# Fourteen instead of twelve chunk pairs in a seven-product down projection, with the rooms, the issue order and the final-norm products rearranged around it

## The chip, the cores and the metric

The kernel runs on one core of one Trainium2 chip. The metric is the device time in microseconds (us) of one execution; the figure given for a kernel is the median of its runs. The engines are TensorE (PE, matrix products; PEld is its weight load), VectorE (DVE, elementwise), ScalarE (ACT, elementwise with functions), GpSimd (POOL) and SyncE (SP); here SP issues most of the loads from memory and POOL issues a few.

## The reference

The reference is one decoder layer over 272 tokens (16 learned ones and 256 of input) of 2048 features. Cut to what matters here:

```python
h = h + y @ w_out                          # after attention and retention
u = rmsnorm(h, ffn_norm)
g = causal_conv3(u @ w_gate)               # 2048 -> 5632
a = silu(g) * (u @ w_up)                   # 5632 features
h = h + a @ w_down                         # 5632 -> 2048, "down"
out = rmsnorm(h, final_norm)[last 256 tokens]
```

All of it is float32. The kernel gets that accuracy from a reduced-precision matrix type by splitting each operand into a high and a low half and adding three products: high by high, high by low, low by high.

## The kernel before, in words

The work runs in stages: 48 input projections with attention and retention beside them, 16 output projections, then "gate and up" (for each of the NF = 44 chunks of 128 features one gate product and one up product, with convolution, silu and the product of the two), and last "down". Every weight chunk is loaded by SP into a `raw` tile (five places, used in turn, L166 to L172). `prep` (L191) then makes its two halves: ACT copies the weight to the high half (L206, tiles `whi`), DVE subtracts that from the weight to give the low half (L207, tiles `wlo`). There are four places for such a pair of halves: three of `whi`/`wlo` and one called `wx`. So part n of the weights can be split only when PE is done with part n-4. PE uses the halves in L872, L873 and L874.

Down multiplies 2 halves of the tokens (m = 0, 1; 128 tokens each) by 44 feature chunks by 4 column blocks of 512. It does the column blocks two at a time, in two groups g = 0, 1; a group holds its partial sums in the eight banks of PSUM. There are two ways to do the feature chunks of a group:

* A plain part `W` is two feature chunks for one column block: 1024 weight columns to split, and 4 products of 512 columns (2 token halves by 2 chunks).
* A pair of feature chunks is done with seven products of 128x128x512 instead of eight, as in Strassen's method for two-by-two blocks. The weights of a pair come as four parts: `d` (two blocks as loaded, two products), `u` (two sums of blocks, two products), `t` (the two blocks of `d`, each less one of the sums, two products) and `c` (one block, called B11, one product). So a pair splits 3584 weight columns, and DVE also does the subtraction of 1024 columns that makes `t` (L218).

NS = 12 pairs cover feature chunks 0 to 23; the other 20 are plain. `down_order` (L96) writes the order of a group out by hand: some plain parts first (4 in group 0, 2 in group 1), then the 48 parts of the pairs with plain parts spread evenly between them, then the rest of the plain parts (3 in group 0, 8 in group 1). The last HOLD = 6 plain parts of group 1 are held: they are multiplied for the first token half, then for the second, so that the first half's result can be finished meanwhile.

What a pair needs beside the weights is made in the gate and up stage. `stage` (L777) loads three weight blocks of a pair on POOL's queue into a tile `ts`, `sums` (L786) makes the two sums `td` of them with two DVE instructions and stores them to memory. For each pair of chunks, L831 to L843 make sums of activations, split them and store them to memory (`sd`). In down, the load of a pair (L174 to L184) issues four transfers on SP, in this order: the two blocks of `d`, the activation sums `sf`, the sums `td`, and B11 (`sw`). `sf` and `sw` each have two rooms, used in turn by even and odd pairs; a room is part of the memory that held the activations of the earlier stage (`act2a` to `act3b`).

At each part, `ahead` (L229) issues the loads of chunks that open up to 6 parts later and the splits of parts up to 3 later, then the products follow, and then `pump` takes one task from the list `side` (three at a time behind the last pair). Those tasks are the additions of the PSUM banks into the result `htok` (L925), the squares for the final norm (`square`, L893, on ACT), the products with the final norm's weights (`weigh`, L899, on DVE), and the load (`norm`, L853, on POOL's queue, a transfer of 512 KB) and scaling (`norm_scale`, L859) of these weights for one group's columns. Before the change, the tasks that finish group 0 run among the first parts of group 1: four squares, four `weigh`, then `norm(1)` and, 12 parts later, `norm_scale(1)`.

The order in which each engine gets its instructions is settled when the kernel is built: the compiler's scheduler takes the instructions by their place in the program, but lets one go ahead when it expects an earlier one to wait. Instructions inside `keep(...)` stay in the order of the program among themselves. On the chip, each engine then takes its instructions strictly in that order.

Of the kernel before, what the change touches and what calls it, by code (L numbers as in the profile page):

```python
# [44 lines left out]
LAM_INIT = 0.8 - 0.6 * math.exp(-0.3 * 0)  # L45
HK = KT // 2
HOLD = 6
NS = 12
KP = 2 * NS
NPL = (NF - KP) // 2  # L50
LEAD = [(4, 3), (2, HOLD + 2)]
PARTS = ("d", "u", "t", "c")
ROOMS = (0, 1, "2a", "2b", "3a", "3b")
RSEQ = [("y", 0), ("g", 0), ("y", 1), ("g", 1), ("y", 2), ("y", 3), ("g", 2), ("g", 3)]


# [60 lines left out]
def trunk_kernel(ctx, tc, a, out):  # L117
# [48 lines left out]
    def load(c):  # L166
        turn = (c - nw) % 5 if c >= nw else 0
        if turn == 3:
            t = pools["dn"].tile([P, D], F32, tag="sraw", name=f"raw{c}")
        elif turn == 4:  # L170
            t = big.tile([P, D], F32, tag="act1", name=f"raw{c}")
        else:  # L172
            t = wp.tile([P, D], F32, tag="raw", bufs=3, name=f"raw{c}")
        if c in mixed:  # L174
            g, p = divmod(mixed[c], NS)
            sf = big.tile([P, 6 * P], F32R, tag=f"act{2 + p % 2}a", name=f"sf{g}_{p}")
            sw = big.tile([P, NW], F32, tag=f"act{2 + p % 2}b", name=f"sw{g}_{p}")
            w = a["w_mix"][g, p]
            keep(nc.sync.dma_start(out=t[:, :2 * NW], in_=w[:, :2 * NW]))
            keep(nc.sync.dma_start(out=sf.bitcast(F32), in_=pools["sd"][p]))  # L180
            keep(nc.sync.dma_start(out=t[:, 2 * NW:], in_=pools["td"][g, p]))
            keep(nc.sync.dma_start(out=sw, in_=w[:, 2 * NW:3 * NW]))
            pools["sf"][g, p] = sf
            pools["sw"][g, p] = sw  # L184
        else:
            ins = nc.sync.dma_start(out=t, in_=chunks[c])
            if c >= nw:
                keep(ins)
        raw[c] = t

    def prep(hf):  # L191
        c, s = entries[hf]
        held = len(entries) - 1 - hf
        if held < 2:
            hi, lo = [big.tile([P, 1024], F32R, tag=f"act{2 + held}{i}", name=f"end{held}{i}")
                      for i in "ab"]
        elif c >= nw and (hf - 2 * nw) % 4 == 3:
            wx = big.tile([P, 2 * 1024], F32R, tag="act0", name=f"wx{hf}")
            hi, lo = wx[:, :1024], wx[:, 1024:]
        else:  # L200
            hi = wp.tile([P, 1024], F32R, tag="whi", bufs=3, name=f"whi{hf}")
            lo = wp.tile([P, 1024], F32R, tag="wlo", bufs=3, name=f"wlo{hf}")

        def halves(src, b, e):
            with tc.high_priority() if 8 < hf < 16 else nullcontext():
                S.copy(out=hi[:, b:e], in_=src)  # L206
                V.tensor_tensor(out=lo[:, b:e], in0=src, in1=hi[:, b:e].bitcast(F32),  # L207
                                op=ALU.subtract)

        if c in mixed:  # L210
            g, p = divmod(mixed[c], NS)
            if s == "d":
                halves(raw[c][:, :2 * NW], 0, 2 * NW)
            elif s == "u":
                halves(raw[c][:, 2 * NW:], 0, 2 * NW)
                two = raw[c][:, :2 * NW].rearrange("p (a c) -> p a c", a=2)
                t2 = raw[c][:, 2 * NW:3 * NW].unsqueeze(1).to_broadcast([P, 2, NW])
                V.tensor_tensor(out=two, in0=two, in1=t2, op=ALU.subtract)  # L218
            elif s == "t":
                halves(raw[c][:, :2 * NW], 0, 2 * NW)  # L220
            else:
                halves(pools["sw"][g, p], 0, NW)
        else:
            halves(raw[c][:, s * 1024:(s + 1) * 1024], 0, 1024)
        pairs[hf] = (hi, lo)
        if s in (1, PARTS[-1]):
            raw.pop(c)
# [536 lines left out]
    with ExitStack() as p2:  # L764
# [27 lines left out]
            stage()  # L792

        for f in range(NF):
            if f in (1, 2):
                stage()
            if staged and (f >= KP or f >= 4 and f % 2 == 0):
                sums()
            if f in (39, 41):
                m = (f - 39) // 2  # L800
                halfs.append(big.tile([P, D], F32, tag=f"htok{m}", name=f"htok{m}"))
                keep(nc.sync.dma_start(out=halfs[m], in_=hd[m * P:(m + 1) * P]))
            ps = gemm_q(idx, gs, 0)
# [56 lines left out]
            keep(V.tensor_scalar(out=fns[g], in0=fns[g], scalar1=-0.5, scalar2=None,  # L860
                                 op0=ALU.mult))

        norm(0)
        side.extend([nop] * 12 + [lambda: norm_scale(0)])
        so = sp.tile([P, 2, NB + 1], F32, name="so", bufs=1)
        pre = sp.tile([P, 2], F32, name="pre", bufs=1)
        root = sp.tile([P, 1], F32, name="root", bufs=1)
# [60 lines left out]
        for g in range(2):  # L928
# [42 lines left out]

                return [f1, f2, f3, f4, f5]

            def finish(m, j):
                n = 2 * g + j

                def f():
                    square(m, n * NW, (n + 1) * NW, n)
                    weigh(m, n * NW, (n + 1) * NW)
                return f  # L980

            def take(m, j):
                def f():
# [6 lines left out]
            for i, (kind, x, y) in enumerate(seq):  # L990
                ahead(e)
                if g and i >= len(seq) - HOLD:
                    held.append((y, e))
                    e += 1
                    continue
                wt = pairs[e]
                if kind == "w":
                    for m in range(2):
                        for kk in range(2):
                            product((m, x % 2), acts(m, KP + 2 * y + kk), wt, kk * NW)  # L1000
                elif y == "d":
                    product((0, 0), acts(0, 2 * x + 1), wt, 0)
                    product((0, 1), forms(x, 2), wt, NW)
                elif y == "u":
                    product(6, forms(x, 0), wt, 0)
                    product(7, forms(x, 1), wt, NW)
                elif y == "t":
                    product((1, 0), acts(1, 2 * x + 1), wt, 0)
                    product(5, acts(1, 2 * x), wt, NW)
                else:  # L1010
                    product(1, acts(0, 2 * x), wt, 0)
                pairs.pop(e)
                e += 1
                if i == last_s:
                    side.extend(joined())
                    side.extend([take(0, 0), take(1, 0)])
                    if g:
                        side.extend([finish(0, 0), finish(1, 0)])
                        side.append(lambda: S.activation(out=root, in_=so[:, 1, 2:3],
                                                         func=AF.Sqrt))  # L1020
                pump(3 if i > last_s else 1)
            pump(len(side))
            if not g:
                take(0, 1)()
                take(1, 1)()
                side.extend([nop] * 6)
                for m, j in ((0, 0), (1, 0), (0, 1), (1, 1)):
                    side.extend([finish(m, j), nop, nop])
                side.append(lambda: norm(1))
                side.extend([nop] * 12 + [lambda: norm_scale(1)])  # L1030
                continue
            po = [bank[0, 1], bank[1, 1]]
            nb = NPL
# [121 lines left out]
```

## Time and profile before

| | |
|---|---|
| median of 3 runs | 1151.01 us (1151.01 to 1151.01) |
| profiled execution | 1151.3 us, its span 1149.5 us |
| PE busy | 1138.5 us, 99% of the span |
| DVE busy | 931.0 us, 81% |
| ACT busy | 605.6 us, 53% |
| POOL busy | 36.2 us, 3% |
| moved by DMA | 276.76 MB, mean 241 GB/s |

The span runs from the first to the last instruction that the profile shows; 1.8 us of the execution's own time lie outside it. "Busy" is the time in which an engine has an instruction in work; instructions of one engine can overlap a little at their ends, so the distance from one start to the next is shorter than an instruction's duration. In a list of waits, each row tells which engine and line waited, for whom, how long in total, how many times, and the longest. In a list by stretches, each engine's busy time stands with the number of its instructions in brackets.

### The profile page before, as it was taken

Reading aid. Unit: us, or ns where it says so; the run is one execution under the profiler, and the core shown is the slowest. Engines: PE = TensorE matmul, PEld = TensorE weight load, DVE = VectorE, ACT = ScalarE, POOL = GpSimd, SP = SyncE. Lnnn points to the kernel's source line nnn. Section 1 sums busy time; section 2 is a strip of 40 time slices with the busy share of each in tenths; the row PEclk is TensorE's granted clock in tenths of the full one; section 3 lists DMA queues with packets and bytes.
Section 4 is the critical chain, followed back from the end, with each engine's and each line's share of the span. In section 5 each row is a group of like instructions: output and inputs, shape, how many; then the busy total and the mean of one; then the engine's idle time right before and its main releaser. Section 6 shows DMA issues by size and latency. Waiting matters only on the chain.

```text
span 1149.5 us, 20662 instructions
## 1 busy us (share of the span) xinstructions
PE 1138.5 (99%) x7967; PEld 1065.6 (93%) x7967; DVE 931.0 (81%) x1738; ACT 605.6 (53%) x997; POOL 36.2 (3%) x84
## 2 busy tenths in 40 slices
PE   8999999999999999999999999999999999999997
PEld 7999999999999999999999999999999988888886
DVE  7898787667677769888888888888877778889996
ACT  7676665443345545444544444444444456656663
POOL 0000000000000000000000000100000000000000
PEclk9999999999999999999999999999999999999999
DMA  9644546565648875767867777888876588877981
GB/s 317 211 155 161 180 144 199 167 223 166 203 159 253 238 228 187 284 243 256 288 249 251 273 286 266 289 313 304 310 271 226 193 302 300 287 287 259 315 314 74
DMA packets 96018, 276.76 MB, mean 241 GB/s; under 512 B 43856, under 2 KB 52176, under 8 KB 74160
## 3 DMA queue, kind: packets, MB, share of 16 engines
q1 hardware_dynamic: 87616, 238.08, 59.9%
q0 software_dynamic: 8160, 37.23, 8.9%
q8 instruction: 62, 1.02, 0.3%
q14 instruction: 36, 0.29, 0.1%
q10 hardware_dynamic: 144, 0.14, 0.1%
HBM read 251.56 MB, written 23.86 MB: 240 GB/s over the span
## 4 chain that ended last, share of the span: by engine, by line
PE 98%; DMA 1%; ACT 0%; DVE 0%; issue 0%; SPq 0%; DVEq 0%; ACTq 0%
PE mm L459 14%; PE mm L448 10%; PE mm L446 10%; PE mm L447 10%; PE mm L438 7%; PE mm L439 7%; PE mm L440 7%; PE mm L461 7%; PE o L873 4%; PE o L874 4%; PE o L872 4%; PE x L872 2%; PE x L874 2%; PE x L873 2%; PE po L583 1%; DMA xr<-in_x_dram 1%
## 5 line engine op out<-in xcount | busy, mean ns | idle before, releaser
L206 ACT CAST whi<-raw 128x1024 fp32r<-128x1024 f32 x379 | 397.9, 1051 | 376.3 <-issue 90.7
L207 DVE TENSOR_TENSOR wlo<-raw,whi 128x1024 fp32r<-128x1024 f32 x379 | 462.0, 1222 | 131.6 <-ACT whi L206 124.7
L459 PE MATMUL mm<-g,whi 128*128 128x512 f32 x352 | 124.4, 392 | 0.0
L448 PE MATMUL mm<-g,wlo 128*128 128x258 f32 x352 | 99.4, 282 | 0.0
L438 PE MATMUL mm<-x,whi 128*128 128x272 f32 (+1 forms) x344 | 99.3, 289 | 0.0
L446 PE MATMUL mm<-g,whi 128*128 128x260 f32 x352 | 99.2, 282 | 0.0
L440 PE MATMUL mm<-x,wlo 128*128 128x272 f32 (+1 forms) x344 | 99.0, 288 | 0.0
L439 PE MATMUL mm<-x,whi 128*128 128x272 f32 (+1 forms) x344 | 98.9, 288 | 0.0
L461 PE MATMUL mm<-g,wlo 128*128 128x256 f32 x352 | 98.6, 280 | 0.0
L447 PE MATMUL mm<-g,whi 128*128 128x256 f32 x352 | 97.8, 278 | 0.0
L459 PEld LDWEIGHTS mm<-g,whi 128*128 128x128 f32 x352 | 66.1, 188 | 13.1
L446 PE MATMUL mm<-ys,whi 128*128 128x260 f32 x256 | 71.9, 282 | 0.0
L448 PE MATMUL mm<-ys,wlo 128*128 128x258 f32 x256 | 71.8, 281 | 0.0
L447 PE MATMUL mm<-ys,whi 128*128 128x256 f32 x256 | 70.7, 276 | 0.0
L447 PEld LDWEIGHTS mm<-g,whi 128*128 128x128 f32 x352 | 66.7, 189 | 1.9
L461 PEld LDWEIGHTS mm<-g,wlo 128*128 128x128 f32 x352 | 66.2, 188 | 0.0
L446 PEld LDWEIGHTS mm<-g,whi 128*128 128x128 f32 x352 | 66.1, 188 | 0.0
L448 PEld LDWEIGHTS mm<-g,wlo 128*128 128x128 f32 x352 | 66.0, 188 | 0.0
L439 PEld LDWEIGHTS mm<-x,whi 128*128 128x128 f32 x344 | 64.9, 189 | 0.0
L440 PEld LDWEIGHTS mm<-x,wlo 128*128 128x128 f32 x344 | 64.8, 189 | 0.0
L438 PEld LDWEIGHTS mm<-x,whi 128*128 128x128 f32 x344 | 64.8, 188 | 0.0
L873 PE MATMUL o<-wlo,fhi 128*128 128x512 f32 x149 | 58.0, 389 | 0.0
(404 smaller groups left out, 3060.6 us busy)
## 6 DMA issues: line engine op xcount, KB each, us to landing
raw<-in_w_in_dram SPq DMA_DIRECT2D x44, 1024.0 KB, 5.0
raw<-in_w_gate_dram SPq DMA_DIRECT2D x44, 1024.0 KB, 5.7
raw<-in_w_up_dram SPq DMA_DIRECT2D x44, 1024.0 KB, 5.4
raw<-in_w_down_dram SPq DMA_DIRECT2D x20, 1024.0 KB, 8.4
ts<-in_w_mix_dram POOLq DMA_DIRECT2D x24, 768.0 KB, 5.9
raw<-in_w_out_dram SPq DMA_DIRECT2D x16, 1024.0 KB, 5.3
td<-ts POOLq DMA_DIRECT2D x24, 512.0 KB, 6.6
raw<-in_w_mix_dram SPq DMA_DIRECT2D x24, 512.0 KB, 8.3
```

The costliest lines, as they stand in the source:

```text
L206: S.copy(out=hi[:, b:e], in_=src)
L207: V.tensor_tensor(out=lo[:, b:e], in0=src, in1=hi[:, b:e].bitcast(F32), op=ALU.subtract)
L438: PE.matmul(ps[:, :n], wh, xh, start=(k == 0), stop=False)
L439: PE.matmul(ps[:, :n], wh, xl, start=False, stop=False)
L440: PE.matmul(ps[:, :n], wl, xh, start=False, stop=(k == KT - 1))
L446: PE.matmul(ps[:, :NQ + 2], wh, src.cols(k, GO - 2, GL), start=(k == 0), stop=False)
L447: PE.matmul(ps[:, 4:NQ + 2], wh, src.cols(k, GL, GW), start=False, stop=False)
L448: PE.matmul(ps[:, 2:NQ + 2], wl, src.hi(k), start=False, stop=(k == KT - 1))
L459: PE.matmul(ps, wh, src.cols(k, GO + 2, GW), start=(k == 0), stop=(k == KT - 1))
L461: PE.matmul(ps[:, :SEQ], wl, src.cols(k, GO + 2, GL), start=False, stop=False)
L872: PE.matmul(o, ah, wh, start=start, stop=False)
L873: PE.matmul(o, ah, wl, start=False, stop=False)
```

## The change

`NS` goes from 12 to 14: fourteen pairs, so 28 chunks are paired and 16 are plain. A group then has 56 parts of pairs and 16 plain parts; in group 0 these are 4 in front, 9 between and 3 behind, in group 1 they are 2, 6 and 8.

Around that, four things are rearranged. The activation sums `sf` take three rooms in turn (`act2a`, `act2b`, `act3a`), and the two places of B11 are the halves of one tile in the fourth (`act3b`). The subtraction that makes part `t` moves in the program from behind the split of `u` to behind the split of `d`. In gate and up, the weight sums start at f = 2 and are made at three of every four chunks, and the two loads of the token rows (`htok`) are issued at f = 41 and 42 instead of 39 and 41. And the products with the final norm move: `norm(0)` is issued 24 parts into group 0 instead of before it, the squares of group 0 still run early in group 1, but its four `weigh`, `norm(1)` and `norm_scale(1)` come behind the last pair of group 1.

```diff
-NS = 12
+NS = 14
+FORMS = ("2a", "2b", "3a")
...
             g, p = divmod(mixed[c], NS)
-            sf = big.tile([P, 6 * P], F32R, tag=f"act{2 + p % 2}a", name=f"sf{g}_{p}")
-            sw = big.tile([P, NW], F32, tag=f"act{2 + p % 2}b", name=f"sw{g}_{p}")
+            n = mixed[c]
+            sf = big.tile([P, 6 * P], F32R, tag="act" + FORMS[n % 3], name=f"sf{g}_{p}")
+            if "b11" not in pools:
+                pools["b11"] = big.tile([P, 2, NW], F32, tag="act3b", name="b11")
+            sw = pools["b11"][:, n % 2]
...
             if s == "d":
                 halves(raw[c][:, :2 * NW], 0, 2 * NW)
-            elif s == "u":
-                halves(raw[c][:, 2 * NW:], 0, 2 * NW)
                 two = raw[c][:, :2 * NW].rearrange("p (a c) -> p a c", a=2)
                 t2 = raw[c][:, 2 * NW:3 * NW].unsqueeze(1).to_broadcast([P, 2, NW])
                 V.tensor_tensor(out=two, in0=two, in1=t2, op=ALU.subtract)
+            elif s == "u":
+                halves(raw[c][:, 2 * NW:], 0, 2 * NW)
...
         for f in range(NF):
-            if f in (1, 2):
+            if f < 2:
                 stage()
-            if staged and (f >= KP or f >= 4 and f % 2 == 0):
+            elif staged and f % 4 != 3:
                 sums()
-            if f in (39, 41):
-                m = (f - 39) // 2
+            if f in (41, 42):
+                m = f - 41
...
-        norm(0)
-        side.extend([nop] * 12 + [lambda: norm_scale(0)])
+        side.extend([nop] * 24 + [lambda: norm(0)] + [nop] * 12 + [lambda: norm_scale(0)])
...
-            def finish(m, j):
-                n = 2 * g + j
-
-                def f():
-                    square(m, n * NW, (n + 1) * NW, n)
-                    weigh(m, n * NW, (n + 1) * NW)
-                return f
+            def squared(m, n):
+                return lambda: square(m, n * NW, (n + 1) * NW, n)
+
+            def weighed(m, n):
+                return lambda: weigh(m, n * NW, (n + 1) * NW)
...
                 if i == last_s:
+                    if g:
+                        side.extend([weighed(m, n) for n in range(2) for m in range(2)])
+                        side.append(lambda: norm(1))
                     side.extend(joined())
                     side.extend([take(0, 0), take(1, 0)])
                     if g:
-                        side.extend([finish(0, 0), finish(1, 0)])
+                        side.append(lambda: norm_scale(1))
+                        for m in range(2):
+                            side.extend([squared(m, 2), weighed(m, 2)])
                         side.append(lambda: S.activation(out=root, in_=so[:, 1, 2:3],
                                                          func=AF.Sqrt))
...
                 side.extend([nop] * 6)
-                for m, j in ((0, 0), (1, 0), (0, 1), (1, 1)):
-                    side.extend([finish(m, j), nop, nop])
-                side.append(lambda: norm(1))
-                side.extend([nop] * 12 + [lambda: norm_scale(1)])
+                for m, n in ((0, 0), (1, 0), (0, 1), (1, 1)):
+                    side.extend([squared(m, n), nop, nop])
                 continue
```

## The prediction, made before the changed kernel was built

> **What bounds the kernel now.** I read the page first: the span, the busy lines and the chain of work that ended last.
>
> ```profile
> span 1149.5 us, 20662 instructions
> PE 1138.5 (99%) x7967; PEld 1065.6 (93%) x7967; DVE 931.0 (81%) x1738; ACT 605.6 (53%) x997; POOL 36.2 (3%) x84
> PE 98%; DMA 1%; ACT 0%; DVE 0%; issue 0%; SPq 0%; DVEq 0%; ACTq 0%
> ```
>
> PE carries 98% of the chain, so what counts is how many matrix products PE has and where it waits. The change touches two stages, so the second view is busy time by stretches: gate and up with activation sums (420 to 689) and without (689 to 880), then down: the pairs of group 0 (919 to 1010), the pairs of group 1 (1033 to 1115.25), and from the last pair to the end of the first token half (1115.25 to 1135.40). The two rows of 20 us are parts of group 1.
>
> ```profile
> core 0: us, PE busy (x) PEld busy (x) DVE busy (x) ACT busy (x) POOL busy (x), PEclk, DMA share, GB/s
> 420.00:689.00 269.00, 269.00 (x1922) 252.99 (x1921) 222.37 (x413) 129.83 (x216) 17.17 (x32) 1.00 0.71 256
> 689.00:880.00 191.00, 191.00 (x1361) 179.52 (x1360) 156.68 (x255) 88.33 (x138) 14.39 (x27) 1.00 0.80 289
> 919.00:1010.00 91.00, 91.00 (x403) 75.37 (x402) 75.90 (x73) 54.01 (x59) 0.53 (x1) 1.00 0.85 301
> 1000.00:1020.00 20.00, 20.00 (x90) 16.57 (x89) 17.12 (x17) 13.59 (x15) 0.00 (x0) 1.00 0.92 352
> 1033.00:1115.25 82.25, 82.07 (x359) 66.76 (x358) 74.19 (x73) 52.78 (x59) 0.53 (x1) 1.00 0.84 297
> 1040.00:1060.00 20.00, 19.92 (x87) 15.96 (x86) 19.42 (x22) 12.09 (x14) 0.53 (x1) 1.00 0.82 299
> 1080.00:1100.00 20.00, 19.91 (x87) 15.82 (x86) 19.14 (x19) 12.51 (x15) 0.00 (x0) 1.00 0.94 324
> 1115.25:1135.40 20.15, 20.15 (x100) 17.04 (x99) 18.16 (x25) 11.05 (x15) 0.00 (x0) 1.00 0.16 53
> ```
>
> PE never pauses in gate and up or in group 0. In group 1 it does: two stretches of 20 us hold 87 matrix products where full ones hold 90, and there DVE is busy for over 19 of 20 us. The third view, the waits in down, names them; the three PEld rows (1.7 us in all) are the same in the answer for group 1's pairs alone, so all of them lie there.
>
> ```profile
> ACT whi L206 <- PE o L874: 25.6, 20, 2.5
> ACT whi L206 <- PE x L874: 16.1, 23, 2.2
> ACT whi L206 <- DVE raw L218: 10.7, 7, 2.5
> PEld x L872 <- ACT whi L206: 0.9, 2, 0.5
> ACT end1a L206 <- DMA raw<-in_w_down_dram: 0.8, 1, 0.8
> PEld x L872 <- ACT wx L206: 0.5, 1, 0.5
> ACT wx L206 <- DMA raw<-in_w_down_dram: 0.4, 1, 0.4
> PEld o L872 <- ACT whi L206: 0.3, 1, 0.3
> SPq L180 <- PE x L874: 112.5, 21, 14.0
> ```
>
> ACT mostly waits for PE to free one of the four places (harmless: that is the lead), seven times for the subtraction L218, and hardly for a load. So down is a race: PE first, DVE close behind, with a lead of at most four parts.
>
> **The unit prices.** PE and DVE rows from the timeline; the first two rows are the first product of a plain part and that of the part behind it.
>
> ```profile
> 924.85 0.39 PE L872 MATMUL o<-wx,fhi 128*128 128x512 f32 x1
> 927.57 0.39 PE L872 MATMUL o<-whi,fhi 128*128 128x512 f32 x1
> ...
> 1042.40 0.68 DVE L899 TENSOR_TENSOR htok<-htok,fn 128x512 f32<-128x512 f32 x1
> ...
> 1048.24 1.22 DVE L207 TENSOR_TENSOR wlo<-raw,whi 128x1024 fp32r<-128x1024 f32 x1
> 1049.38 0.68 DVE L207 TENSOR_TENSOR wx<-sw,wx 128x512 fp32r<-128x512 f32 x1
> 1049.98 0.68 DVE L899 TENSOR_TENSOR htok<-htok,fn 128x512 f32<-128x512 f32 x1
> 1050.58 2.35 DVE L207 TENSOR_TENSOR wlo<-raw,whi 128x1024 fp32r<-128x1024 f32 x2
> ...
> 1057.52 0.68 DVE L899 TENSOR_TENSOR htok<-htok,fn 128x512 f32<-128x512 f32 x1
> ...
> 1079.80 0.69 DVE L860 TENSOR_SCALAR fn<-fn 128x1024 f32<-128x1024 f32 x1
> ```
>
> From start to start: a plain part of 12 matrix products takes 2.72 us, so one takes 0.2267. A split of 1024 columns takes DVE 1.14 (1048.24 to 1049.38), one of 512 columns, or a product with the norm, 0.60. I price the subtraction of 1024 columns and the scaling like the rows of their length, 1.14 and 0.60. A pair is then 21 x 0.2267 = 4.76 us of PE and 4 x 1.14 + 0.60 = 5.16 us of DVE; a plain part is 2.72 of PE and 1.14 of DVE. Pairs run DVE behind, plain parts let it catch up.
>
> **The products saved.** Two more pairs in two groups save one product of three matrix instructions each: 12 x 0.2267 = **2.72 us** off PE. The Trainium skill's page "TensorE: Matmul & The Clock Gate", section "Back-to-back issue gap", gives a sustained spacing of 131 ns at 512 columns. By that the saving would be an estimated 1.57 us and the sum 1.1 us worse; these rows are 227 ns apart in a stretch without a wait, and the row decides.
>
> **What pays for it.** DVE work against PE time, over the pairs and the plain parts between them ("room" is what PE's time leaves DVE):
>
> * group 0 before: 12 pairs, 13 plain: PE 92.5, DVE 76.7 + 0.6 (scaling) = 77.3; DVE's room 15.2
> * group 0 after: 14 pairs, 9 plain: PE 91.1, DVE 82.5 + 0.6 = 83.1; room 8.0
> * group 1 before: 12 pairs, 10 plain: PE 84.3, DVE 73.3 + 3.0 (four `weigh`, one scaling) = 76.3; room 8.0
> * group 1 after: 14 pairs, 6 plain: PE 83.0, DVE 79.1; room 3.9
>
> The idle time of DVE measured in group 1 is 82.25 - 74.19 = 8.06, close to the 8.0. A room of 15.2 cost PE nothing, a room of 8.0 cost it 1.7.
>
> Group 1 after: at least 0 new wait, since the work fits. At most: if DVE again loses the same share to waiting (8.06 of 82.25, 9.8%), it needs 79.1 / 0.902 = 87.7, which is 4.7 more than PE has. Seven microseconds of room less brought 1.7 of waiting; 4.1 less again should bring at least as much for each, so 1.7 + 1.0 = 2.7, and more as the room runs out. I take **3.2**. Group 0 after: its room is that of group 1 before, so between 0 and 1.7. Both slow stretches of 20 us have the norm's work in or just in front of them (L899 four times, the first at 1042.40 and the last at 1057.52; L860 at 1079.80), and group 0 has one scaling, so I take **0.6**. The existing waits of **1.7** are counted off, since both groups are priced anew.
>
> The subtraction moved ahead of `u` is part of these figures, not a term beside them. It removes seven waits of ACT (10.7 us) behind which DVE had nothing to split; but no PE wait names L218, so alone it is worth 0 to 1.7. It also puts 1.14 us in front of `u`'s split; queued behind it on DVE are `u`, `t` and `c`, and PE waits for `u` where the lead is already spent. That is a cost of 0 to 1.14 in each pair without lead, and one reason for taking 3.2 and not 2.7.
>
> **The end.** Four `weigh` and one scaling, 5 x 0.60 = 3.0 us, move behind the last pair. Rows of the end before, and the landing of the final-norm transfer:
>
> ```profile
> 1135.38 0.69 DVE L1041 TENSOR_TENSOR htok<-o,htok 128x512 f32<-128x512 f32 x1 [1.99 <-PE o L874]
> ...
> 1141.72 0.42 DVE L1060 TENSOR_TENSOR htok<-oe,htok 128x256 f32<-128x256 f32 x1 [1.47 <-PE oe L874]
> ...
> DMA to landing us min/median/max: 8.2/8.4/8.6
> ```
>
> DVE has 1.99 us free before the first token half's sum, so 1.0 of the 3.0 is over, and all 3.0 if DVE arrives late; behind it 1.47 us are free again before the second half's last sum, which starts the chain to the end. Bounds 0 and 3.0 - 1.47 = 1.5; I take **0.6**. `norm(1)` now waits on POOL for the fourth `weigh` (nothing is queued behind it there) and lands 8.6 us later; DVE has ten additions (6.0) and about six splits (6.8) to do before the scaling that needs it, so it waits for nothing. Of the last loads, the second-last chunk now waits for the place of the last plain chunk among the pairs and the last one is queued behind it on SP, where before only the last one waited so (and ACT 0.8 for it); PE comes to them more than three plain parts later (10.9 us), and the loads in this stage's rows, here and below, land in 4.8 to 8.6: 0, at worst 1.
>
> **What is hidden.** Costs in gate and up and of the transfers:
>
> ```profile
> L789 DVE TENSOR_TENSOR ts<-ts 128x512 f32<-128x512 f32 x24 | 16.5, 687 | 0.5
> L841 DVE TENSOR_TENSOR sh<-sm,sh 128x384 fp32r<-128x384 f32 x12 | 6.6, 548 | 0.0
> L834 DVE TENSOR_TENSOR sm<-ful,sm 128x128 f32<-128x128 f32 x12 | 3.4, 284 | 0.0
> raw<-in_w_mix_dram SPq DMA_DIRECT2D x24, 512.0 KB, 8.3
> raw<-td SPq DMA_DIRECT2D x24, 512.0 KB, 5.8
> sf<-sd SPq DMA_DIRECT2D x24, 384.0 KB, 4.8
> sw<-in_w_mix_dram SPq DMA_DIRECT2D x24, 256.0 KB, 6.5
> ```
>
> Four more weight sums (each this row and its sister L788, alike: 1.37) and two more pairs' activation sums (each about 0.55 + 6 x 0.28) are 10 us of DVE in stretches where it idles 46.6 and 34.3 us and PE never waits; sums at three chunks of four instead of two raise DVE there from 83% to 86%. POOL's transfers, 4 loads and 6 stores more, and the `htok` loads two chunks apart become one apart, on queues that PE does not wait for: 0, and the 10 us in full only if DVE's lead were gone. In down a pair loads 1664 KB and a plain part 512 KB, so group 1 goes from 25.1 to 26.4 MB and 297 to 317 GB/s; the trace has a stretch at 352. Three rooms take away most of the 112.5 us that SP waits for a place of `sf`; as ACT waited 1.2 us for loads and PE never, that is worth 0. `norm(0)` behind 24 parts lands in 8.6 us, and 12 parts last longer: 0.
>
> **The sum**: -2.72 - 1.7 + 3.2 + 0.6 + 0.6 = 0.0. The profiled execution takes 1151.3 (1149.5 of span), 0.3 above the median of 1151.01; at the median I predict **1151.0 us**.
>
> **The rivals.** *The lead holds*: with the subtraction early, the norm's work away and the loads further ahead, DVE loses little, 1.0 in group 1, 0 in group 0 and 0.3 at the end: with -2.72 - 1.7 = -4.42 it is -4.42 + 1.3 = -3.1, **1147.9**. For it: the work fits with 3.9 us to spare, and 1.7 us of present waiting can go. Against: DVE idled 8.06 us in group 1 though it was needed.
>
> *DVE becomes the bound of group 1*, slower: it keeps losing 9.8% to the chain of place, high half, low half, so 4.7 there, 1.7 in group 0, and it comes late to the end, 1.5: -4.42 + 7.9 = +3.5, **1154.5**. It decides from 4.42 + 2.3 = 6.7 us of new waits on. For it: the stretches with over 19 of 20 us busy are just those where PE waits, and the engines' order is fixed in advance, so a misjudged instruction holds up all behind it. Against: part of that idle time is DVE being ahead.
>
> *DVE is the bound already*: then each of the four pairs costs 5.16 - 2 x 1.14 = 2.88 us, 11.5 in all, **1162.5**. The Trainium skill, "Perfetto Trace Analysis", section "Identifying the Most-Contended Engine", would have it so: judge TensorE by its weight loads, here 66.76 of 82.25 (81%), and VectorE by occupancy, here 90%. The trace disagrees: PE's products follow each other without a gap but for 1.7 us.
>
> **How the numbers follow.** Chances: forecast 0.57, lead holds 0.18, DVE the bound 0.23, bound already 0.02. A measurement of this kernel can tell 0.2%, 2.3 us, from no change; the forecast's own range is 1148.7 to 1153.3, that is "same". Faster is the second case, 0.18; slower the last two, 0.25. The range to hold 8 in 10 reaches from the second case's time to the third's: 1148.0 to 1154.6.
>
> **What would show it.** Right: 12 products fewer at 0.227 us; waits of PE for ACT's halves in group 1 of 2 to 4.5 us and under 1.7 in group 0; DVE busy above 93% between group 1's first and last pair; DVE's free time before the first half's sum gone. The waits of ACT for L218 should fall well below 10.7 and SP's for `sf` below 112.5 without moving the time by themselves. Wrong: PE waiting for DVE in gate and up, ACT waiting for loads by more than a few us, or group 1 of pairs with PE waits under 1 us (then faster) or over 5 (then slower).

## The result, and the profile after

The changed kernel takes 1160.92 us (median of 6 runs, 1160.72 to 1161.05), the kernel before in the same series 1151.01 us (6 runs). The ratio is 1.0084, with a 95% interval from 1.0073 to 1.0094: slower by 9.9 us where no change was predicted, and outside the range. The profiled execution of after takes 1161.0 us, its span 1159.2. Two executions at a low granted clock are left out of the ratios below: one of e6 (1879.4 us at 0.557) and one of the kernel before, in the series of e5 to e8 (2215.5 us at 0.935).

The page of after, its span, its busy lines and its chain:

```profile
span 1159.2 us, 20731 instructions
...
PE 1141.7 (98%) x7955; PEld 1062.3 (92%) x7955; DVE 948.0 (82%) x1770; ACT 611.0 (53%) x1009; POOL 41.7 (4%) x94
...
PE 92%; DVE 4%; ACT 2%; issue 1%; DMA 1%; SPq 0%; DVEq 0%; ACTq 0%
```

The twelve matrix products are gone (7967 to 7955), but DVE and ACT now hold 6% of the chain that PE held nearly alone. The first and the last product of down, before and then after:

```profile
916.66 0.39 PE L872 MATMUL o<-whi,fhi 128*128 128x512 f32 x1
...
1141.41 0.28 PE L874 MATMUL oe<-end0a,flo 128*128 128x256 f32 x1
```

```profile
916.52 0.39 PE L875 MATMUL o<-whi,fhi 128*128 128x512 f32 x1
...
1150.92 0.28 PE L877 MATMUL oe<-end0a,flo 128*128 128x256 f32 x1
```

Down went from 224.75 us to 234.40, so the whole loss lies there; what comes ahead of it is no later (916.52 against 916.66) and what comes behind its last product is 0.25 longer. With twelve products fewer it should have been 2.72 shorter: some 12.4 us of new waiting. Below, "PE's waits" are this kind of sum: how much further apart than 0.227 us (0.119 for products half as wide) the starts of consecutive products of down lie, in the profiled execution (differences under 0.03 us are left out). It is 1.1 us before and 13.1 after: 2.6 in group 0, 10.5 from group 1 on.

The stretches of after that answer to those of the prediction (the columns are the same), and one more, 1025 to 1120, which holds nearly the whole of group 1's pairs; then that stretch in the kernel before:

```profile
919.00:1010.00 91.00, 89.97 (x390) 72.42 (x390) 78.82 (x77) 55.64 (x62) 0.54 (x1) 1.00 0.85 306
1033.00:1115.25 82.25, 78.16 (x329) 60.31 (x328) 70.64 (x67) 48.66 (x56) 0.00 (x0) 1.00 0.81 277
1025.00:1120.00 95.00, 90.91 (x384) 70.73 (x383) 82.79 (x83) 56.28 (x68) 0.00 (x0) 1.00 0.77 268
```

```profile
1025.00:1120.00 95.00, 94.82 (x415) 77.29 (x414) 86.94 (x88) 60.68 (x71) 0.53 (x1) 1.00 0.76 269
```

This is not the picture of a DVE that became the bound. In group 1, PE does 31 products fewer in the same 95 us, and DVE is busy for less of it than before, 82.8 us against 86.9, though it has more to do. That is 87% of the stretch, where the prediction expected above 93%. PE and DVE both wait. The waits of after in down, from 905 us to the end, name the place (the last two rows are SP's own queue):

```profile
ACT whi L210 <- DVE raw L220: 28.7, 15, 3.0
...
PEld o L875 <- ACT whi L210: 8.4, 14, 1.3
...
PE o L875 <- ACT whi L210: 3.2, 7, 0.8
PEld o L876 <- DVE wx L211: 1.7, 1, 1.7
...
PEld oe L875 <- DVE htok L928: 1.6, 1, 1.6
...
SPq L186 <- DVE wlo L211: 85.0, 18, 15.0
...
SPq L184 <- PE x L877: 7.9, 7, 3.0
```

The lines have moved by two to four: L210 and L211 are the high and the low half, L220 the subtraction, L875 to L877 the products, L928 the additions, L184 and L186 the loads of the activation sums and of B11. SP no longer waits for a room of the sums (7.9 us, before 112.5), as predicted, though it now stands 85.0 for a place of B11. But ACT's waits for the subtraction, which should have fallen well below 10.7 us, rose to 28.7. The timeline of after shows one of them:

```profile
1069.42 2.36 DVE L211 TENSOR_TENSOR wlo<-raw,whi 128x1024 fp32r<-128x1024 f32 x2 [1.19 <-ACT whi L210]
...
1070.76 1.05 ACT L210 CAST whi<-raw 128x1024 fp32r<-128x1024 f32 x1
...
1071.70 0.69 DVE L211 TENSOR_TENSOR wx<-b,wx 128x512 fp32r<-128x512 f32 x1
...
1072.30 1.22 DVE L211 TENSOR_TENSOR wlo<-raw,whi 128x1024 fp32r<-128x1024 f32 x1
...
1073.44 1.22 DVE L220 TENSOR_TENSOR raw<-raw 128x1024 f32<-128x1024 f32 x1
...
1074.77 2.94 ACT L210 CAST whi<-raw 128x1024 fp32r<-128x1024 f32 x3 [2.96 <-DVE raw L220]
...
1075.84 2.36 DVE L211 TENSOR_TENSOR wlo<-raw,whi 128x1024 fp32r<-128x1024 f32 x2 [1.19 <-ACT whi L210]
1075.86 0.19 PEld L875 LDWEIGHTS o<-whi,fhi 128*128 128x128 f32 x1 [1.26 <-ACT whi L210]
1075.86 0.50 PE L875 MATMUL o<-whi,fhi 128*128 128x512 f32 x1 [0.84 <-ACT whi L210]
```

The second half of the first row is this pair's `d`, split by 1071.78. The subtraction could start then. DVE splits a `c` (1071.70) and the pair's `u` (1072.30) first, and only at 1073.44 subtracts. So `t` is ready for ACT at 1074.66. ACT has stood for 2.96 us by then, with the casts of the next two parts queued behind `t` (the three follow each other without a wait). While ACT casts `t`, DVE has nothing to split and stands 1.19 us; PE runs dry and stands about 1.

In the trace of after the subtraction stands behind `u`'s split in 16 of the 28 pairs (5 in group 0, 11 in group 1; "late" below), in the trace of before in 8 of 24. In the program of after it stands ahead of `u` in all 28. The move in the program did not reach the engine (e8 shows this by undoing it).

### The profile page after: what moved, and what is told of

Read it like the earlier page. It is cut to its first block, busy times and chain, and to the rows that moved or that the text cites. A ratio compares the mean times of both kernels' runs of the same rounds, so it can differ in the third digit from the quotient of the medians.

```text
span 1159.2 us, 20731 instructions
## 1 busy us (share of the span) xinstructions
PE 1141.7 (98%) x7955; PEld 1062.3 (92%) x7955; DVE 948.0 (82%) x1770; ACT 611.0 (53%) x1009; POOL 41.7 (4%) x94
## 4 chain that ended last, share of the span: by engine, by line
PE 92%; DVE 4%; ACT 2%; issue 1%; DMA 1%; SPq 0%; DVEq 0%; ACTq 0%
PE mm L463 14%; PE mm L452 10%; PE mm L450 10%; PE mm L451 10%; PE mm L442 7%; PE mm L443 7%; PE mm L444 7%; PE mm L465 7%; PE o L875 3%; PE o L876 3%; PE o L877 3%; PE x L875 2%; PE x L876 1%; PE x L877 1%; DVE wlo L211 1%
## 5 line engine op out<-in xcount | busy, mean ns | idle before, releaser
L210 ACT CAST whi<-raw 128x1024 fp32r<-128x1024 f32 x383 | 401.2, 1051 | 377.1 <-issue 90.2
L211 DVE TENSOR_TENSOR wlo<-raw,whi 128x1024 fp32r<-128x1024 f32 x383 | 467.2, 1223 | 130.3 <-ACT whi L210 124.6
L463 PEld LDWEIGHTS mm<-g,whi 128*128 128x128 f32 x352 | 66.1, 188 | 13.1
L821 ACT COPY ful<-mm 128x256 f32<-128x256 f32 x44 | 16.4, 373 | 78.2 <-PE mm L463 75.7
```

What stands on the lines that cost most here:

```text
L463: PE.matmul(ps, wh, src.cols(k, GO + 2, GW), start=(k == 0), stop=(k == KT - 1))
```

## The experiments

Two theories went into them. **Order**: the time is lost behind late subtractions. **Room**, the prediction's own: DVE's work comes so near to PE's time that any order would lose. Where "held" is said, the instructions are wrapped in `keep`, so that the scheduler leaves them in the order of the program.

| kernel | late subtractions | PE's waits, us | median, us | ratio to before (95%) |
|---|---|---|---|---|
| before | 8 of 24 | 1.1 | 1151.0 to 1151.5 | 1 |
| after | 16 of 28 | 13.1 | 1160.92 | 1.0084 (1.0073 to 1.0094) |
| e1, held ahead | 0 of 28 | 1.9 | 1149.72 | 0.9986 (0.9977 to 0.9995) |
| e2, 12 pairs | 6 of 24 | 0.2 | 1150.27 | 0.9990 (0.9981 to 0.9999) |
| e3, norm products later | 16 of 28 | 14.1 | 1162.87 | 1.0098 (1.0085 to 1.0112) |
| e4, `t` set free | 28 of 28 | 0.7 | 1147.81 | 0.9972 (0.9961 to 0.9984) |
| e5, held behind | 28 of 28 | 23.5 | 1171.42 | 1.0174 (1.0160 to 1.0188) |
| e6, e1 and more work for DVE | 0 of 28 | 11.4 | 1159.61 | 1.0070 (1.0054 to 1.0086) |
| e7, before, held ahead | 0 of 24 | 1.3 | 1150.29 | 0.9992 (0.9983 to 1.0001) |
| e8, move undone in the program | 16 of 28 | 13.2 | 1161.22 | 1.0085 (1.0066 to 1.0104) |
| e9, e1 with the old norm places | 0 of 28 | 3.8 | 1151.46 | 1.0000 (0.9991 to 1.0009) |
| e10, e1 with two rooms | 0 of 28 | 5.1 | 1153.63 | 1.0018 (1.0009 to 1.0027) |
| e11, e1 with e3's edit | 0 of 28 | 3.4 | 1151.17 | 0.9998 (0.9989 to 1.0007) |
| e12, before, held behind | 24 of 24 | 16.2 | 1169.78 | 1.0159 (1.0142 to 1.0176) |

### e1: the subtraction held ahead of `u`

```diff
-        def halves(src, b, e):
+        def halves(src, b, e, pin=lambda ins: ins):
...
-                V.tensor_tensor(out=lo[:, b:e], in0=src, in1=hi[:, b:e].bitcast(F32),
-                                op=ALU.subtract)
+                pin(V.tensor_tensor(out=lo[:, b:e], in0=src, in1=hi[:, b:e].bitcast(F32),
+                                    op=ALU.subtract))
...
-                V.tensor_tensor(out=two, in0=two, in1=t2, op=ALU.subtract)
+                keep(V.tensor_tensor(out=two, in0=two, in1=t2, op=ALU.subtract))
...
-                halves(raw[c][:, 2 * NW:], 0, 2 * NW)
+                halves(raw[c][:, 2 * NW:], 0, 2 * NW, keep)
```

> The changed kernel with one thing added: the subtraction and u's low split are held in the order in which the program writes them, so that in all 28 pairs the subtraction runs on DVE ahead of u's split (in the changed kernel it ran behind it in 16 of 28). Theory 'order': the new waits are those behind a late subtraction, where ACT cannot cast t; with the subtraction always early PE's waits in down fall from 13 us to 4 or less, ACT's waits for L220 fall from 28.7 us to under 6, and the time is 1150 to 1153.5. Theory 'room': DVE is too full with 28 pairs, whatever the order; the waits only move to u's split, PE's waits stay at 11 to 14 us and the time at 1159 to 1162.

1149.72 us: 11.2 less than after with the same instructions, and 0.14% less than before. The three stretches of this kernel:

```profile
919.00:1010.00 91.00, 91.00 (x401) 74.70 (x400) 81.71 (x79) 57.37 (x62) 0.53 (x1) 1.00 0.89 319
1033.00:1115.25 82.25, 82.07 (x357) 66.05 (x356) 78.24 (x74) 56.42 (x62) 0.00 (x0) 1.00 0.82 296
1025.00:1120.00 95.00, 94.82 (x413) 76.62 (x412) 90.81 (x89) 64.73 (x75) 0.00 (x0) 1.00 0.76 274
```

DVE is now busy for 90.8 of 95 us where after had 82.8, and PE is full. The fuller DVE is the better one. The same pair in the timeline of this kernel:

```profile
1066.15 1.23 DVE L211 TENSOR_TENSOR wlo<-raw,whi 128x1024 fp32r<-128x1024 f32 x1 [0.44 <-ACT whi L210]
...
1067.41 1.23 DVE L220 TENSOR_TENSOR raw<-raw 128x1024 f32<-128x1024 f32 x1
...
1068.55 1.22 DVE L211 TENSOR_TENSOR wlo<-raw,whi 128x1024 fp32r<-128x1024 f32 x1
1068.67 2.21 ACT L210 CAST whi<-raw 128x1024 fp32r<-128x1024 f32 x2
...
1070.29 3.49 DVE L211 TENSOR_TENSOR wlo<-raw,whi 128x1024 fp32r<-128x1024 f32 x3
```

The subtraction follows the split of `d` at once, ACT casts `t` from 1068.67 without a wait, and DVE spends that time on `u` and `c`. The same 1.14 us of DVE now run beside ACT's work instead of in front of it. The expectation that ACT's waits for L220 fall under 6 us was missed, but PE's waits are 1.9 all the same:

```profile
ACT whi L210 <- DVE raw L220: 9.9, 10, 1.5
```

### e2: twelve pairs with the other edits kept

```diff
-NS = 14
+NS = 12
```

> The changed kernel with 12 pairs a group instead of 14; the three rooms, the moved subtraction and the moved norm products stay. Both theories ('order' and 'room') put the loss on the four pairs: 1149 to 1152, PE's waits in down 1 to 4 us. Above 1155 it would be the other edits that cost the time.

1150.27 us, PE's waits 0.2. So the rooms, the norm's move and the moved subtraction are not what costs; the loss appears only with the four pairs.

### e3: the norm products behind the last additions

```diff
                     if g:
-                        side.extend([weighed(m, n) for n in range(2) for m in range(2)])
-                        side.append(lambda: norm(1))
                     side.extend(joined())
                     side.extend([take(0, 0), take(1, 0)])
                     if g:
+                        side.extend([weighed(m, n) for n in range(2) for m in range(2)])
+                        side.append(lambda: norm(1))
```

> The changed kernel with the four moved norm products and the load of the final norm placed behind the ten additions of the last plain part instead of ahead of them. If the pause of 1.4 us in front of the last half's products (PE waiting for an addition to free its PSUM bank) comes from these four products standing in front of the additions, it goes, and the time is 1159.0 to 1159.8; if DVE is late there anyway because of the pairs, 1160.5 to 1161.5 and the pause stays.

1162.87 us: slower than after, both expectations missed. The pause in front of the last half's products is gone, but at 1142.07 PE waits 2.2 us for a low half. DVE's timeline of this kernel says why:

```profile
1136.73 1.22 DVE L211 TENSOR_TENSOR end1b<-raw,end1a 128x1024 fp32r<-128x1024 f32 x1
1137.86 1.22 DVE L211 TENSOR_TENSOR end0b<-raw,end0a 128x1024 fp32r<-128x1024 f32 x1
1139.00 0.68 DVE L902 TENSOR_TENSOR htok<-htok,fn 128x512 f32<-128x512 f32 x1
1139.60 0.68 DVE L928 TENSOR_TENSOR htok<-x,htok 128x512 f32<-128x512 f32 x1
1140.20 0.68 DVE L928 TENSOR_TENSOR t<-x,t 128x512 f32<-128x512 f32 x1
1140.80 1.22 DVE L211 TENSOR_TENSOR wlo<-raw,whi 128x1024 fp32r<-128x1024 f32 x1
```

The split that PE needs next (`wlo`, 1140.80) stands behind the splits of the last two parts (`end1b`, `end0b`), which PE needs later, and behind a norm product. Here too the order of the instructions sets the wait.

### e4: `t` set free of the subtraction

```diff
-                two = raw[c][:, :2 * NW].rearrange("p (a c) -> p a c", a=2)
-                t2 = raw[c][:, 2 * NW:3 * NW].unsqueeze(1).to_broadcast([P, 2, NW])
-                V.tensor_tensor(out=two, in0=two, in1=t2, op=ALU.subtract)
             elif s == "u":
                 halves(raw[c][:, 2 * NW:], 0, 2 * NW)
+                done = raw[c][:, 2 * NW:]
+                V.tensor_tensor(out=done, in0=raw[c][:, :2 * NW], in1=done, op=ALU.subtract)
```

> The changed kernel with as much work for DVE, but t's split no longer depends on the subtraction: the subtraction, behind u's split in every pair, writes over u's columns, which nobody reads any more, and t is split from the blocks as loaded (so the part 'less the third block' of t is left out of what is computed). Theory 'order' (the wait for the subtraction costs the time): PE's waits in down 5 us or less, 1148 to 1153. Theory 'room' (DVE's amount of work costs it): unchanged, PE's waits 11 to 14 us, 1159 to 1162.

1147.81 us with PE's waits at 0.7: as many DVE instructions of the same size, all 28 of them behind `u`, and 13 us less than after. (`t` is here left without its subtraction, so this kernel does not compute the reference.) What costs is that `t` has to wait for the instruction, not that DVE has to do it.

### e5: held behind `u` in all pairs

The subtraction is written back behind `u`'s halves, with e1's `keep`.

```diff
             if s == "d":
                 halves(raw[c][:, :2 * NW], 0, 2 * NW)
-                (subtraction)
             elif s == "u":
-                halves(raw[c][:, 2 * NW:], 0, 2 * NW)
+                halves(raw[c][:, 2 * NW:], 0, 2 * NW, keep)
+                keep(subtraction)
```

> The changed kernel with the subtraction held behind u's low split in all 28 pairs (in the changed kernel 16 of 28, in the run with it held ahead 0 of 28). Theory 'order': each late subtraction costs PE about (13.05 - 1.88) / 16 = 0.70 us, so 28 cost about 19.5 over the run with none: 1163 to 1173, with ACT's waits for the subtraction at 45 us or more. Rival 'mixture': it is only the irregular order of the changed kernel, early in one pair and late in the next, that costs; regular late ones are planned around: 1150 to 1157.

1171.42 us. With 0, 16 and 28 late subtractions the same kernel takes 1149.72, 1160.92 and 1171.42: 0.70 us on the mean for each of the first 16, 0.88 for each of the next 12. A regular late order is as bad as a mixed one.

### e6: more work for DVE, order held

```diff
                 halves(raw[c][:, 2 * NW:], 0, 2 * NW, keep)
+                done = raw[c][:, 2 * NW:3 * NW]
+                keep(V.tensor_tensor(out=done, in0=done, in1=done, op=ALU.add))
```

> The kernel with the subtraction held ahead of u (1149.7) and one more DVE instruction of 512 columns (0.60 us) behind u's split in each of the 28 pairs; its output is read by nobody. It takes 8.4 us of DVE's room in each group: 8.0 becomes -0.4 in group 0 and 3.9 becomes -4.5 in group 1. Theory 'order' (with the right order room can be used up to the last): PE waits about what DVE's work is over PE's time, 0.4 + 4.5 on top of 1.9, so 1153.5 to 1157.5. Theory 'room' (DVE cannot use the last 8 us of its room whatever the order): nearly all 16.8 us land on PE, 1163 to 1167.

1159.61 us, 9.9 more than e1: between the two expectations. PE's waits rose by 2.4 in group 0, where the added work takes the room to -0.4, and by 7.2 from group 1 on, where it is -4.5. One stretch of it:

```profile
1025.00:1120.00 95.00, 90.56 (x389) 71.66 (x387) 92.84 (x97) 58.77 (x69) 0.00 (x0) 1.00 0.76 273
```

This is what a DVE that is the bound looks like: 92.8 of 95 us busy while PE waits. So the amount of DVE's work does cost once it is more than PE's time: with the order held, the prediction's table of room gives the right scale, with two to three us a group that come on top. It could not show what a late instruction costs.

### e7 and e12: the same two orders in the kernel before

e7 is the kernel before with the subtraction held ahead of `u` (e1's edit and the move), e12 with it held behind (e1's `keep` alone).

> The kernel before (24 pairs, old rooms, old norm products) with nothing changed but the subtraction held ahead of u's split (before: behind it in 8 of 24). Theory 'order': most of the 1.1 us of PE's waits go, 1149.8 to 1150.8; nothing more, since PE hardly waits otherwise. If the subtraction ahead of u's split cost PE something by itself (1.14 us in front of u where the lead is spent), 1151.5 to 1154.

> The kernel before (24 pairs) with the subtraction held behind u's split in all 24 pairs (before: 8). With 28 late pairs PE waited 7.4 us in group 0 (room 8.0) and 16.0 from group 1 on (room 3.9), with none late 0.4 and 1.5: 0.50 and 1.04 us for each late one. 'Order alone' (a late subtraction costs the same at any room): 0.77 each on the mean, 24 x 0.77 = 18.5, so 1166 to 1171. 'Order and room' (what a late one costs depends on the room of its group): group 1 has room 8.0 here, so 12 x 0.50 = 6.0, and group 0 with 15.2 between 0 and 3: 1155.5 to 1160.

e7 takes 1150.29 us, which can't be told from before, and PE's waits stay at 1.3. So the 8 late subtractions of before cost nothing that shows, and the ones held ahead cost nothing either. e12 takes 1169.78, inside the range of "order alone": with room of 15.2 and 8.0, 24 late ones cost (1169.78 - 1151.54) / 24 = 0.76 us each, as in e5, where the rooms are 8.0 and 3.9 ((1171.42 - 1149.72) / 28 = 0.78). Part of this may not be the order's: three executions of e12 ran at a granted clock of 0.995 (1169.6 to 1170.2), and the fourth, the profiled one, at 0.998, like the kernel before, takes 1166.67, which is 0.63 for each late one.

In group 0, where PE never paused before, it now waits 4.4 us. PE's waits by group, less those of the kernel with none late (e7 and e1), give the price of one late subtraction: in e12 0.37 us in group 0 (room 15.2) and 0.88 from group 1 on (room 8.0), in e5 0.50 (room 8.0) and 1.04 (room 3.9). So "order alone" is right only for the whole: in the same group a late one costs a little less where there is more room. But "order and room", which put group 1 of e12 at 0.50 as well, is wrong too, since the same room of 8.0 goes with 0.50 in one group and 0.88 in the other. What else differs between the groups was not tried. The waits of e12 in down:

```profile
DVE wlo L207 <- ACT whi L206: 25.8, 30, 1.6
ACT whi L206 <- DVE raw L218: 22.9, 11, 3.3
...
PEld o L872 <- ACT whi L206: 9.3, 14, 1.3
...
PEld o L872 <- ACT wx L206: 7.1, 10, 1.6
```

DVE waits 25.8 us for ACT and ACT 22.9 for DVE: a chain between the two, which DVE's spare time does not take away.

### e8: the move undone in the program

```diff
             if s == "d":
                 halves(raw[c][:, :2 * NW], 0, 2 * NW)
-                (subtraction)
             elif s == "u":
                 halves(raw[c][:, 2 * NW:], 0, 2 * NW)
+                (subtraction)
```

> The changed kernel with the subtraction written back behind u's halves in the program (nothing held). If the move in the program does not reach the engines: the subtraction runs behind u's split in 16 of 28 pairs as before it is written back, and the time is that of the changed kernel, 1160 to 1162. If the move does something: another count, and another time by 0.7 us for each pair.

1161.22 us and again 16 late ones; in the two traces the instructions of every engine, DVE's 1770 and PE's 7955 among them, stand in the same order from the first to the last. This part of the change does nothing to the kernel: whether the subtraction is written ahead of `u` or behind it, it is issued in the same place.

### e9, e10, e11: the other edits, with the order held

e9 puts the norm's products, loads and scalings back (`finish` and the lists as in the kernel before), e11 makes e3's edit in e1, and e10 takes two rooms:

```diff
-            sf = big.tile([P, 6 * P], F32R, tag="act" + FORMS[n % 3], name=f"sf{g}_{p}")
+            sf = big.tile([P, 6 * P], F32R, tag="act" + FORMS[2 * (n % 2)], name=f"sf{g}_{p}")
```

> The kernel with the subtraction held ahead of u (1149.7), but the norm products, the scalings and the loads of the final norm back in their old places (28 pairs stay). That puts four products and a scaling, 3.0 us of DVE, back among group 1's pairs, whose room falls from 3.9 to 0.9. From the run with an added instruction (room -0.4 in group 0 cost 2.8 of PE's waits, room -4.5 in group 1 cost 5.8) a room of 0.9 should cost 2 to 3 instead of the 1.5 of now: 1150.2 to 1151.5. If room does not count until it is used up: 1149.2 to 1150.2. If the move of the products is what made 28 pairs possible: 1152 or more.

> The kernel with the subtraction held ahead of u (1149.7), with the activation sums in two rooms instead of three (the third stays empty). The prediction put the three rooms at 0: SP's waits for a place of sf rise from 3.7 us to over 30 and the time stays, 1149.2 to 1150.3. If the transfers further ahead are needed by 28 pairs, ACT waits for loads and the time is 1151 or more.

> The kernel with the subtraction held ahead of u (1149.7) and the four norm products behind the ten additions of the last plain part. In the changed kernel this cost 2 us more (1162.9), there with DVE late by then. If that came from DVE being late: 1149.2 to 1150.3, no pause of PE behind the last pair. If the place by itself costs: 1151 to 1152.5.

e9 takes 1151.46 us, 1.7 more than e1, with 3.5 us of PE's waits from group 1 on instead of 1.5: with the order held, the room of group 1 does count, and the move of the norm products is worth those 1.7 us. e10 takes 1153.63 (1152.0 to 1155.9), 3.9 more. Its waits:

```profile
SPq L184 <- PE x L877: 110.5, 24, 16.4
...
ACT whi L210 <- DMA raw<-in_w_down_dram: 4.2, 3, 2.8
ACT whi L210 <- DMA raw<-td: 2.6, 3, 1.0
...
PE o L875 <- ACT whi L210: 2.2, 1, 2.2
ACT wx L210 <- DMA raw<-td: 1.4, 1, 1.4
```

SP stands 110.5 us for a room, as it did before, but with 28 pairs the loads queued behind it now come too late: ACT waits 8.2 us for loads, and PE 2.2 at once. PE's waits, from the profiled executions, are 3.2 us above e1's. The median's 3.9 holds more than that: the four runs of e10 at a granted clock of 0.999 lie between 1152.0 and 1153.0, and the slowest of all ran at 0.996. e11 takes 1151.17, 1.4 more than e1, with one pause of 1.4 us for a low half, as in e3. So that place costs by itself, and not only where DVE is late already; the expectation of no change was wrong.

e1 is the fastest kernel that computes the reference: 0.14% under the kernel before, with an interval that stays below 1; e2 and e7 can't be told from it.

## Why the prediction was wrong

**The products saved** (2.72): right. 12 products are gone at 0.227 us each.

**Gate and up, 0**: right. Down starts at 916.66 before and 916.52 after, and no wait of PE for DVE shows in that stage.

**The subtraction's move**: the step that failed first. The prediction took it that the subtraction is issued ahead of `u` because the program writes it there, called its effect "part of these figures", and bounded it by a gain of 0 to 1.7 and a cost of 0 to 1.14 in each pair without lead. In the trace 16 of 28 stand behind `u`, and e8 shows that the move reaches no engine. The description of the kernel before says that the scheduler may let an instruction go ahead when it expects an earlier one to wait. That fits: the subtraction overwrites `d` and has to wait for `d`'s split, while `u` has to wait for its own cast alone. That this is the scheduler's reason is argued, not shown.

**New waits of group 1 (3.2, bounds 0 to 4.7) and group 0 (0.6, bounds 0 to 1.7)**: far too small. They came to 2.6 in group 0 and 7.8 in group 1's pairs, with 2.7 behind 1120 us (the 1.7 of before that was counted off is idle time of the weight load; by the starts of the products it was 1.1); the prediction had named over 5 us in group 1 as what would prove it wrong. The method failed, not a number in it: room compares sums of work, and the upper bound let the waits scale with DVE's idle share. e4 does the same amount of work with 0.7 us of waits, e1 with 1.9, after with 13.1; e12 has twice the room and waits 16.2. The waits come from the chain subtraction, cast of `t`, split of `t`, and when it starts is set by where the subtraction stands. The row that spoke of it was there: ACT waited seven times, 2.5 us at most, for L218. The prediction dismissed it because no PE wait named L218. For the kernel before that was no error in the time, since e7 takes the late ones away and gains nothing that shows; the step that failed was to carry it over to 28 pairs. There PE's waits name ACT and ACT's name the subtraction, so a wait has to be followed for two steps before it is dismissed.

**Three rooms, 0**: wrong with 28 pairs. e10 puts the third room at 3.2 us of PE's waits, 3.9 by the medians. The prediction argued from the kernel before, where 112.5 us of SP's waits cost nothing; with four pairs more, 1664 KB each, they do cost. Against the kernel before it is no gain, as the sum had it, but without the third room four more pairs did not pay even with the order held (1153.63).

**The end (0.6, bounds 0 to 1.5)**: mis-sized, and for the most part by the same cause. 1.3 us go in one pause, PE waiting for an addition (L928) to free its bank, and 0.25 behind the last product. In DVE's timeline of after that addition (1137.69) stands behind both of the last parts' splits:

```profile
1134.29 1.22 DVE L211 TENSOR_TENSOR wlo<-raw,whi 128x1024 fp32r<-128x1024 f32 x1
1135.42 1.22 DVE L211 TENSOR_TENSOR end1b<-raw,end1a 128x1024 fp32r<-128x1024 f32 x1
1136.56 1.22 DVE L211 TENSOR_TENSOR end0b<-raw,end0a 128x1024 fp32r<-128x1024 f32 x1
1137.69 0.69 DVE L928 TENSOR_TENSOR htok<-o,htok 128x512 f32<-128x512 f32 x1
```

In e1, whose program is the same there, PE's waits behind 1120 us are 0, and only the 0.24 behind the last product is left: the pause comes with DVE being late by then, not with the five moved instructions alone. That the load of the final norm would be hidden was right: it is issued at 1133.47 and its scaling waits for nothing.

**The rivals.** "The lead holds" (1147.9) assumed what e1 and e4 enforce, and those two came out at 1149.7 and 1147.8 (e4 without the subtraction in `t`). "DVE becomes the bound of group 1" (1154.5) had the right sign, and among its grounds the right one, a misjudged order that holds up all behind it; but its chain (place, high half, low half) lacks the subtraction, and it priced the loss as a share of DVE's time, 6.4 us short. "DVE is the bound already" (1162.5) is within 1.6 us of the result and yet refuted: e1 gives DVE the same work, by its page 948.8 us against 948.0 in after, and takes 1149.7.

```profile
PE 1137.2 (99%) x7955; PEld 1063.8 (93%) x7955; DVE 948.8 (83%) x1770; ACT 614.0 (53%) x1009; POOL 41.6 (4%) x94
```

The Trainium skill, "Perfetto Trace Analysis", section "Optimization Strategy", tells the reader to find the gaps on the engine that one optimizes for and what blocks it there. The trace agrees: PE's gaps name ACT (8.4 us, 14 times), and followed one step further ACT's name the subtraction (28.7 us, 15 times), which DVE's 82% of the span does not tell.

The sum, from the trace: -2.72 (products), +11.9 (PE's waits, 1.14 to 13.05), +0.5 (starts that lie a few hundredths further apart), +0.25 (the end), -0.14 (down starts earlier) = +9.8, and the spans on the two pages differ by 9.7.

## What to carry to other kernels

Here an order written in the program did not reach the engine until it was held: look in the trace where the moved instruction stands before pricing what the move is worth. Where one engine's output goes to a second and back to the first, price the length of that chain beside the sums of work; spare time on an engine (15.2 us in group 0 of e12) did not pay for an instruction that starts 1.14 us late in such a chain (4.4 us of waits). And a transfer's wait that costs nothing now (112.5 us of SP's before) can cost after the next change (110.5 us in e10).

## What was not expected of the hardware

* A late instruction of 1.14 us costs PE 0.37 to 1.04 us each time where all are late, and doubling DVE's spare time in a group took away only 0.13 to 0.16 of it (e5 and e12). But 8 of 24 in before and 6 of 24 in e2 cost nothing that shows. Which places in a group forgive a late one, and why the scheduler puts 16 late with 28 pairs but 6 with 24, was not tried.
* DVE, with the order held, goes to 90.8 busy us of 95 without PE waiting for more than 0.2 us in that stretch by the busy time (1.5 by the starts), and with work added to 92.8 of 95. In this kernel an engine that is 96% busy was no loss.
* The kernel in which ACT waits for loads (e10) scatters by 3.8 us over its runs (1152.0 to 1155.9); e1, with its loads ahead, by 1.1 (1149.1 to 1150.2). The slower runs of e10 go mostly with a lower granted clock; what makes the scatter is not shown.
